# The low part of every third of the first 32 weight chunks moves from VectorE to GpSimd, in a two-layer encoder on one core

## The chip, the core and the metric
One core of a Trainium2 chip. The metric is device time in microseconds (us) of one execution; the kernel is timed in several runs and the median counts. The engines are TensorE (PE; its weight loads are PEld), VectorE (DVE), ScalarE (ACT), GpSimd (POOL) and SyncE (SP, which only issues transfers here).

## The reference
Two layers over x[256, 1024], 16 heads of 64. Both have the form x <- LayerNorm(ALPHA x + (o * silu(g)) w_out), where q, k, v and g come from one input projection.
```python
# layer 0: an indexer picks 64 keys of each query
rel   = relu(einsum('bqhd,bsd->bqhs', qi, ki) * 64 ** -0.5)
score = where(adm, einsum('bqhs,bqh->bqs', rel, wi), -inf)
_, idx = top_k(score, 64)            # softmax attention over these keys only
# layer 1: stick-breaking attention
a = where(before, exp(log_sigmoid(z) + log_stick), 0)
```
All of it is float32.

## The kernel before, in words
Every float32 operand of a large product is split in two float32r parts, a high part h (a cast) and a low part lo = src - h, and a product is three matmuls: h*h, l*h and h*l. For the weights `split` (L62) does it: ACT casts `wh` (L63), DVE subtracts `wl` (L64).

The weights come as 80 chunks of 128x1024 (512 KB) in a fixed order (`w_all`). `fetch` (L72) takes the next chunk: a DMA on SP's queue into `raw` (a pool of four, `wraw`), then the split into `wh` and `wl` (a pool of eight, `wspl`). `load_chunk` keeps `AHEAD` = 2 chunks fetched beyond the one handed out. A transfer into `raw` can start only when ACT and DVE have read the tile's earlier contents, and SP issues its transfers in order. Chunks 0 to 23 are the q, k and v projections of layer 0 (four chunks each, in the order q, k, v, k, q, v of half a matrix), 24 to 31 the gates of layer 0; then come its output projection and layer 1.

`tok_block` (L119) uses four chunks for two PSUM tiles (256 tokens by 512 columns); a chunk makes 12 matmuls of 512 columns (L107), in the order h*h, l*h, h*l, so that `wl` of a chunk is needed last. The PSUM pool `pp` has three banks. What empties them: `rope` (L191 to L198) on DVE for q and k, a copy into `vt` on ACT (L333) for v. Beside the projections run the indexer's `select` (scores `sc` on L273, from `rel` on ACT, L270; then eight rounds of MAX and MATCH_REPLACE, L279 and L280) and later the heads: `keys0` (transposes L374, then `zh` on ACT and `zl` on DVE, L229 and L230), `logits0` and so on.

The code says what is computed in which program order; a scheduler then orders the instructions of all engines by its own cost estimates. Each engine runs its instructions in that order, so an instruction that waits holds all behind it on its engine. POOL clears and casts some constants at the start (L175 to L188) and takes a power of -0.5 in each LayerNorm (L442).

Of the kernel before, what the change touches and what calls it, by code (L numbers as in the profile page):

```python
# [11 lines left out]
AF = mybir.ActivationFunctionType  # L12
# [13 lines left out]
ALPHA = (2.0 * 2) ** 0.25  # L26
# [2 lines left out]
CW = 1024  # L29
WARM = 8  # L30
AHEAD = 2
IDX_A = 5 * HD
IDX_W = IH * HD + HD + IH
NEG_ADM = -1.0e38
# [8 lines left out]
def trunk(ctx: ExitStack, tc: tile.TileContext, x_rows, x_idx, w_all, consts, lnp, out):  # L43
    nc = tc.nc
# [17 lines left out]
    def split(h, lo, src):  # L62
        nc.scalar.activation(h, src, AF.Copy)  # L63
        nc.vector.tensor_sub(lo, src, as32(h))  # L64

    # activations, feature-major: [feature in tile, tile, token], split in two float32r parts
    xTh = sb.tile([P, KT, S], F32R, name="xTh", tag="aTh")
    xTl = sb.tile([P, KT, S], F32R, name="xTl", tag="aTl")

# [3 lines left out]
    def fetch():  # L73
        c = n_chunk[0]
        if c == w_all.shape[0]:
            return
        n_chunk[0] += 1
        raw = wraw.tile([P, CW], F32, name="raw", tag="raw")
        nc.sync.dma_start(raw, w_all[c])
        wh = wspl.tile([P, CW], F32R, name="wh", tag="wh")  # L80
        wl = wspl.tile([P, CW], F32R, name="wl", tag="wl")
        split(wh, wl, raw)
        ahead.append((wh, wl))

    def load_chunk():
# [8 lines left out]
        return p.tile([P, 512], F32, name="bank", tag="bank")[:, :w]  # L94

    def load_block():
        """A quarter of [1024, 512] of a weight matrix after the other: two K tiles a chunk."""
        for _ in range(4):
            yield [w.rearrange("p (k n) -> p k n", k=2) for w in load_chunk()]

    def tok_part(outs, src, wc, c):
        """Adds a chunk's part to the token tiles in outs (tile, PSUM): the activations are stationary."""
        for xp, wp in ((0, 0), (1, 0), (0, 1)):
            for t, ps in outs:
                for k in range(2):
                    kk = 2 * c + k
                    nc.tensor.matmul(ps, src[kk][xp][:, t * P:(t + 1) * P], wc[wp][:, k, :],  # L107
                                     start=kk == 0 and xp + wp == 0, stop=kk == 7 and wp == 1)

    def tok_block(src):  # L110
        """Yields after every chunk but the last; returns the PSUM tiles."""
        ps = [bank(pp) for _ in range(NT)]
        for c, wc in enumerate(load_block()):
            if c:
                yield
            tok_part(list(enumerate(ps)), src, wc, c)
        return ps

    def mix(*gens):  # L119
        """One step of every generator in turn."""  # L120
        live = list(gens)
        while live:
            for g in list(live):
                try:
                    next(g)
                except StopIteration:
                    live.remove(g)
# [4 lines left out]
        nc.tensor.matmul(ps, sl, mh, start=False, stop=last)  # L132

    def proj_feat(ps, src, chunk):
        """[128 features, 256 tokens]: the weights are stationary."""
        w = [p.rearrange("p (k n) -> p k n", k=KT) for p in chunk]
        for wp, xp in ((0, 0), (0, 1), (1, 0)):
            for k in range(KT):
                nc.tensor.matmul(ps, w[wp][:, k, :], src[k][xp], start=k + xp + wp == 0,  # L139
                                 stop=k == 7 and wp == 1)  # L140

    # the tensor engine's clock comes up while the first loads are under way
    rest = cst.tile([P, 512], mybir.dt.bfloat16, name="rest")
    nc.vector.memset(rest, 0.0)
    idle = bank(pp)
    for _ in range(WARM):
        nc.tensor.matmul(idle, rest[:, :P], rest, start=True, stop=True)

    # ---------------------------------------------------------------- loads
    cuts = (slice(0, IDX_A), slice(IDX_A, IDX_W))  # L150
    idx_w = []
    for k in range(KT):
        raw = wraw.tile([P, CW], F32, name="raw", tag="raw")[:, :S + IDX_W]
        if k:
            nc.sync.dma_start(raw, x_idx[k])
        else:
            first = S + IDX_A
            nc.sync.dma_start(raw[:, :first], x_idx[k, :, :first])
            nc.scalar.dma_start(raw[:, first:], x_idx[k, :, first:])
        wh = wspl.tile([P, CW], F32R, name="wh", tag="wh")[:, :IDX_W]  # L160
        wl = wspl.tile([P, CW], F32R, name="wl", tag="wl")[:, :IDX_W]
# [35 lines left out]
        nc.vector.tensor_add(dst[:, :, :32], a[:, :, :32], b[:, :, 32:])  # L197
        nc.vector.tensor_add(dst[:, :, 32:], a[:, :, 32:], b[:, :, :32])  # L198

    # ---------------------------------------------------------------- layer 0: indexer  # L200
    psi = [[bank(at) for _ in range(2)] for t in range(NT)]
    for k in range(KT):
        w = idx_w[k]
# [33 lines left out]
            r = slice(i * HD, (i + 1) * HD)  # L237
            feat_split(z[0][r, i, :], z[1][r, i, :], src[r, :], scale)

    # indexer: qi of two heads stationary, ki moving, once for either head  # L240
    kz = zpad[0]
    pt = bank(at)
    for t in range(NT):
# [41 lines left out]
            negm.append(nm)  # L285


    # ---------------------------------------------------------------- layer 0: q, k
    qh = [sb.tile([P, S], F32R, name=f"qh{j}", tag=f"ah{j}") for j in range(NPAIR)]
    ql = [sb.tile([P, S], F32R, name=f"ql{j}", tag=f"al{j}") for j in range(NPAIR)]  # L290
    kr = [wk.tile([P, D], F32, name=f"kr{t}", tag="z").rearrange("p (h d) -> p h d", d=HD)
# [47 lines left out]
        yield  # L339

    def weighted_v(j, p0, p1):
        """o^T of two heads from the weights [s, (q)] of either."""
        po = bank(at)
        for i in range(2):
            hs = slice((2 * j + i) * HD, (2 * j + i + 1) * HD)
            rs = slice(i * HD, (i + 1) * HD)
            nc.tensor.matmul(po[rs, :S], vt[0][:, hs], p0(i), start=True, stop=False)  # L347
            nc.tensor.matmul(po[rs, P:S], vt[1][:, hs], p1(i), start=False, stop=True)  # L348
        if j in sg:
            gated(j, po[:, :S], sg.pop(j))  # L350
        else:
            oT[j] = keep(f"oT{j}")
            nc.scalar.activation(oT[j], po[:, :S], AF.Copy)

    def gate(j, src):
        """2 silu(g) = g (1 + tanh(g / 2)) of two heads"""
        ps = bank(pp, S)
        proj_feat(ps, src, load_chunk())
        th = wk.tile([P, S], F32, name="th", tag="og")
        nc.scalar.activation(th, ps, AF.Tanh, scale=0.5)  # L360
        if j in oT:
            nc.vector.scalar_tensor_tensor(th, th, 1.0, ps, op0=OP.add, op1=OP.mult)
            gated(j, oT.pop(j), th)
        else:
            sg[j] = keep(f"sg{j}")
            nc.vector.scalar_tensor_tensor(sg[j], th, 1.0, ps, op0=OP.add, op1=OP.mult)
# [57 lines left out]
    g_b = {}  # L424

    def out_norm(layer, x, after):
        """x[t] = LayerNorm(ALPHA x[t] + (gated o) w_out)"""
        z = [wk.tile([P, D], F32, name="z", tag="z") for _ in range(NT)]
        st = [wk.tile([P, 4, 6], F32, name="st") for _ in range(NT)]

        def residual(t, c0, ps):
            ns = slice(c0, c0 + ps.shape[1])
            nc.vector.scalar_tensor_tensor(z[t][:, ns], x[t][:, ns], ALPHA, ps, op0=OP.mult, op1=OP.add)
            for c in range(ns.start, ns.stop, 256):
                nc.vector.bn_stats(st[t][:, c // 256, :], z[t][:, c:c + 256])

        def norm(t):
            mv = wk.tile([P, 2], F32, name="mv")
            nc.vector.bn_aggr(mv, st[t].rearrange("p a b -> p (a b)"))
            rs = wk.tile([P, 1], F32, name="rs")  # L440
            nc.vector.tensor_scalar(rs, mv[:, 1:2], EPS, None, op0=OP.add)
            nc.gpsimd.tensor_tensor(rs, rs, mhalf, op=OP.pow)  # L442
            for n in range(2):
                ns = slice(n * 512, (n + 1) * 512)
                nc.vector.scalar_tensor_tensor(z[t][:, ns], z[t][:, ns], mv[:, 0:1],
                                               g_b[layer, 0][:, ns], op0=OP.subtract, op1=OP.mult)
                nc.vector.scalar_tensor_tensor(x[t][:, ns], z[t][:, ns], rs, g_b[layer, 1][:, ns],
                                               op0=OP.mult, op1=OP.add)
                after(t, n)

        tiles = [bank(pp) for _ in range(NT)]
        for c, wc in enumerate(load_block()):
            while any(k not in og for k in (2 * c, 2 * c + 1)):
                yield
            tok_part(list(enumerate(tiles)), og, wc, c)
            yield
        for t in range(NT):
            residual(t, 0, tiles[t])
        ws = list(load_block())
        for t in range(NT):  # L460
            for cols in ((0, 512),) if t == 0 else ((0, 256), (256, 512)):
                ps = bank(pp, cols[1] - cols[0])
                for c in range(4):
                    tok_part([(t, ps)], og, [w[:, :, cols[0]:cols[1]] for w in ws[c]], c)
                residual(t, 512 + cols[0], ps)
            norm(t)
        og.clear()
# [15 lines left out]
    x = [sb.tile([P, D], F32, name=f"x{t}", tag=f"x{t}") for t in range(NT)]  # L483
# [27 lines left out]
        pass  # L511
    load_gb(1)

    # ---------------------------------------------------------------- layer 1
    ys = [(yTh[:, k], yTl[:, k]) for k in range(KT)]
    wv = {}
    for t in range(NT):
# [106 lines left out]


def _rows(w):
    """[1024, n] -> [128, 8, n]: the row of a K tile in front."""
    return w.reshape(KT, P, w.shape[1]).transpose(1, 0, 2)


# [51 lines left out]
```

## Time and profile before
| | us |
|---|---|
| timed runs | 317.7, 318.9, 319.74 |
| median | 318.9 |
| span of the profiled execution (the page gives no other time of it) | 318.4 |
| PE, DVE, ACT, POOL busy in the profiled execution | 304.0, 238.5, 186.7, 7.8 |

The span is the time from the first to the last instruction of one profiled execution. Busy time of PE is modelled, so a busy PE is not PE at its peak. All times below count from the span's start. Lines are those of the kernel before; in the changed kernel lines behind the change are 2 to 6 higher (L64 is L66, L333 is L339).

### The profile page before, as it was taken

What the parts mean: (1) busy time and instruction counts of PE and PEld (TensorE: products, weight loads), DVE (VectorE), ACT (ScalarE), POOL (GpSimd) and SP (SyncE); (2) the same over time, 40 slices, a digit from 0 to 9 for tenths busy, and PEclk for the clock granted to TensorE, in tenths of its full rate; (3) what the DMA queues carried; (4) which work ended last, traced back from release to release, by engine and by line L of the source; (5) the groups of instructions that cost most, each with busy time, mean ns of one, the idle gap of its engine ahead of it and who ended that gap; (6) DMA issues with size and microseconds to landing.
All of it is one profiled execution on the core that took longest, in us unless ns stands there. A gap on an engine that the chain in (4) does not pass through costs nothing.

```text
span 318.4 us, 5179 instructions
## 1 busy us (share of the span) xinstructions
PE 304.0 (95%) x1914; PEld 264.2 (83%) x1914; DVE 238.5 (75%) x514; ACT 186.7 (59%) x365; POOL 7.8 (2%) x16
## 2 busy tenths in 40 slices
PE   8997899996999999999999999999999999999990
PEld 5985788885887899987788889999999999987790
DVE  3777999997998899897389667655677767662475
ACT  5655545664336997876306276556698888965200
POOL 3010000000000000000010100000000000000011
PEclk9999999999899999999999999999999999999997
DMA  7799744784233745665422949866543433000003
GB/s 263 249 324 307 271 141 143 236 264 153 59 95 118 258 136 153 193 203 178 134 66 80 294 134 320 282 192 165 189 148 118 110 103 118 2 1 1 2 2 130
DMA packets 14425, 50.44 MB, mean 158 GB/s; under 512 B 1600, under 2 KB 1728, under 8 KB 14400
## 3 DMA queue, kind: packets, MB, share of 16 engines
q1 hardware_dynamic: 14256, 49.97, 48.9%
q8 instruction: 15, 0.25, 0.4%
q10 hardware_dynamic: 144, 0.14, 0.1%
q14 instruction: 10, 0.08, 0.1%
HBM read 49.05 MB, written 1.05 MB: 157 GB/s over the span
## 4 chain that ended last, share of the span: by engine, by line
PE 73%; DMA 11%; DVE 10%; ACT 3%; issue 2%; DVEq 0%; SPq 0%; ACTq 0%
PE bank L139 29%; PE bank L107 28%; DMA raw<-w_all 9%; DVE wl L64 4%; PE bank L347 3%; DMA raw<-x_idx 2%; ACT wh L63 2%; PE bank L348 1%; PE bank L571 1%; PE bank L130 1%; DVE sc L280 1%; PE bank L549 1%; PE bank L548 1%; PE bank L550 1%; PE bank L132 1%
## 5 line engine op out<-in xcount | busy, mean ns | idle before, releaser
L63 ACT ACTIVATE wh<-raw 128x1024 fp32r<-128x1024 f32 (+2 forms) x89 | 90.1, 1015 | 58.9 <-DMA raw<-w_all 25.7
L64 DVE TENSOR_TENSOR wl<-raw,wh 128x1024 fp32r<-128x1024 f32 (+2 forms) x89 | 103.5, 1164 | 28.1 <-ACT wh L63 27.2
L107 PE MATMUL bank<-wh,xTh 128*128 128x512 f32 x96 | 28.6, 411 | 2.6 <-DVE rb L196 2.5
L107 PE MATMUL bank<-wh,xTl 128*128 128x512 f32 x96 | 27.9, 400 | 0.0
L107 PE MATMUL bank<-wl,xTh 128*128 128x512 f32 x96 | 27.5, 395 | 0.0
L139 PE MATMUL bank<-yTh,wh 128*128 128x256 f32 x192 | 27.4, 285 | 0.0
L139 PE MATMUL bank<-yTl,wh 128*128 128x256 f32 x192 | 26.9, 283 | 0.0
L139 PE MATMUL bank<-yTh,wl 128*128 128x256 f32 x192 | 26.9, 283 | 0.0
L139 PEld LDWEIGHTS bank<-yTh,wh 128*128 128x128 f32 x192 | 24.7, 190 | 1.2 <-DVE sl L64 0.7
L139 PEld LDWEIGHTS bank<-yTh,wl 128*128 128x128 f32 x192 | 24.8, 192 | 0.0
L139 PEld LDWEIGHTS bank<-yTl,wh 128*128 128x128 f32 x192 | 24.7, 192 | 0.0
L107 PEld LDWEIGHTS bank<-wh,xTh 128*128 128x128 f32 x96 | 17.8, 194 | 7.3 <-issue 3.6
L107 PEld LDWEIGHTS bank<-wh,xTl 128*128 128x128 f32 x96 | 18.5, 194 | 3.9
L107 PEld LDWEIGHTS bank<-wl,xTh 128*128 128x128 f32 x96 | 18.0, 188 | 3.7
L107 PE MATMUL bank<-wh,oh 128*128 128x512 f32 (+1 forms) x80 | 20.8, 355 | 0.0
L107 PE MATMUL bank<-wh,ol 128*128 128x512 f32 (+1 forms) x80 | 20.5, 352 | 0.0
L107 PE MATMUL bank<-wl,oh 128*128 128x512 f32 (+1 forms) x80 | 20.4, 350 | 0.0
L557 DVE SCALAR_TENSOR_TENSOR ab<-bank,ab 128x512 f32<-128x512 f32 (+1 forms) x16 | 8.2, 553 | 12.8 <-ACT ab L556 12.8
L107 PEld LDWEIGHTS bank<-wl,oh 128*128 128x128 f32 x80 | 14.0, 188 | 2.2
L107 PEld LDWEIGHTS bank<-wh,ol 128*128 128x128 f32 x80 | 13.9, 188 | 2.3 <-issue 0.2
L107 PEld LDWEIGHTS bank<-wh,oh 128*128 128x128 f32 x80 | 13.6, 189 | 2.2 <-issue 0.3
L398 ACT ACTIVATE p<-ml,mx 128x128 f32<-128x128 f32 (+1 forms) x32 | 14.3, 447 | 1.1 <-DVE mx L393 0.6
(148 smaller groups left out, 552.3 us busy)
## 6 DMA issues: line engine op xcount, KB each, us to landing
raw<-w_all SPq DMA_DIRECT2D x80, 512.0 KB, 4.2
raw<-x_idx SPq DMA_DIRECT2D x7, 420.0 KB, 3.9
gb<-lnp SPq DMA_DIRECT2D x4, 512.0 KB, 7.0
x<-x_rows SPq DMA_DIRECT2D x2, 512.0 KB, 6.1
y<-x SPq DMA_DIRECT2D x4, 256.0 KB, 2.1
cs<-consts SPq DMA_DIRECT2D x1, 512.0 KB, 7.0
raw<-x_idx SPq DMA_DIRECT2D x1, 288.0 KB, 3.0
raw<-x_idx ACTq DMA_DIRECT2D x1, 132.0 KB, 3.2
```

The costliest lines, as they stand in the source:

```text
L63: nc.scalar.activation(h, src, AF.Copy)
L64: nc.vector.tensor_sub(lo, src, as32(h))
L107: nc.tensor.matmul(ps, src[kk][xp][:, t * P:(t + 1) * P], wc[wp][:, k, :], start=kk == 0 and xp + wp == 0, stop=kk == 7 and wp == 1)
L130: nc.tensor.matmul(ps, sh, mh, start=first, stop=False)
L132: nc.tensor.matmul(ps, sl, mh, start=False, stop=last)
L139: nc.tensor.matmul(ps, w[wp][:, k, :], src[k][xp], start=k + xp + wp == 0, stop=k == 7 and wp == 1)
L280: nc.vector.match_replace(out=sc, in_to_replace=m8, in_values=sc, imm_value=NEG_REP)
L347: nc.tensor.matmul(po[rs, :S], vt[0][:, hs], p0(i), start=True, stop=False)
L348: nc.tensor.matmul(po[rs, P:S], vt[1][:, hs], p1(i), start=False, stop=True)
L398: nc.scalar.activation(p[:, i, :], m[:, i, :], AF.Exp, bias=mx[:, c], scale=-1.0, accum_out=sm[:, c])
L548: nc.tensor.matmul(pv, kh[:, ks], z[0][:, :, qs], start=True, stop=False)
L557: nc.vector.scalar_tensor_tensor(a, pv, 0.0, a, op0=OP.max, op1=OP.add)
```

## The change
`fetch` splits chunks 2, 5, 8, ... 29 (ten of the first 32) with the subtract on GpSimd instead of VectorE. All other chunks, and the split of activations, stay as they are.
```diff
+SHARED = 32
...
         wh = wspl.tile([P, CW], F32R, name="wh", tag="wh")
         wl = wspl.tile([P, CW], F32R, name="wl", tag="wl")
-        split(wh, wl, raw)
+        if c < SHARED and c % 3 == 2:
+            nc.scalar.activation(wh, raw, AF.Copy)
+            nc.gpsimd.tensor_sub(wl, raw, as32(wh))
+        else:
+            split(wh, wl, raw)
         ahead.append((wh, wl))
```
The scheduler lays out all engines anew. [...]
```order
L188 MEMSET zl1_178 128x512
L175 CAST cr_165<-cs_163 128x384
L442 ISA
L442 TENSOR_TENSOR rs_1918<-rs_1918,mhalf_171 128x1
L442 TENSOR_TENSOR rs_1995<-rs_1995,mhalf_171 128x1
```
Now ten subtracts stand between (chunks 2, 5, 8, 11, 14, 17 are the first six rows of L86):
```order
L194 MEMSET zl1_178 128x512
L181 CAST cr_165<-cs_163 128x384
L86 ISA
L86 TENSOR_TENSOR wl_290<-raw_287,wh_289 128x1024
L86 TENSOR_TENSOR wl_442<-raw_439,wh_441 128x1024
L86 TENSOR_TENSOR wl_552<-raw_549,wh_551 128x1024
L86 TENSOR_TENSOR wl_638<-raw_635,wh_637 128x1024
L86 TENSOR_TENSOR wl_764<-raw_761,wh_763 128x1024
L86 TENSOR_TENSOR wl_818<-raw_815,wh_817 128x1024
```
On ACT, where the first v block ends and its two PSUM banks are copied into `vt0` and `vt1`, there stood (`wh_692` is chunk 13, 763 is 14, 781 is 15, 799 is 16, 817 is 17):
```order
L63 ACTIVATE wh_692<-raw_690 128x1024
L270 ACTIVATE rel_674<-bank_670 128x512
L270 ACTIVATE rel_700<-bank_696 128x512
L63 ACTIVATE wh_763<-raw_761 128x1024
L63 ACTIVATE wh_781<-raw_779 128x1024
L333 ACTIVATE vt0_366<-bank_615 128x512
L333 ACTIVATE vt1_367<-bank_616 128x512
L270 ACTIVATE rel_722<-bank_718 128x512
```
and now stands:
```order
L65 ACTIVATE wh_692<-raw_690 128x1024
L85 ACTIVATE wh_763<-raw_761 128x1024
L276 ACTIVATE rel_648<-bank_644 128x512
L65 ACTIVATE wh_781<-raw_779 128x1024
L276 ACTIVATE rel_674<-bank_670 128x512
L276 ACTIVATE rel_700<-bank_696 128x512
L65 ACTIVATE wh_799<-raw_797 128x1024
L85 ACTIVATE wh_817<-raw_815 128x1024
L339 ACTIVATE vt0_366<-bank_615 128x512
L339 ACTIVATE vt1_367<-bank_616 128x512
L276 ACTIVATE rel_722<-bank_718 128x512
```
The casts of chunks 16 and 17 have moved ahead of the copies, and the `rel` of the second token tile's scores behind the cast of chunk 14. A little later on ACT, where the keys of the second pair of heads are split (`zh1`, first and second half), there stood (`wh_921` is chunk 20, 946 is 21, 1027 is 22, 1045 is 23):
```order
L63 ACTIVATE wh_921<-raw_919 128x1024
L229 ACTIVATE zh1_177<-bank_821 64x256
L63 ACTIVATE wh_946<-raw_944 128x1024
L229 ACTIVATE zh1_177<-bank_821 64x256
L63 ACTIVATE wh_1027<-raw_1025 128x1024
```
and now stands:
```order
L85 ACTIVATE wh_921<-raw_919 128x1024
L65 ACTIVATE wh_946<-raw_944 128x1024
L65 ACTIVATE wh_1027<-raw_1025 128x1024
L235 ACTIVATE zh1_177<-bank_821 64x256
L85 ACTIVATE wh_1045<-raw_1043 128x1024
L235 ACTIVATE zh1_177<-bank_821 64x256
```
Here too the casts of two further chunks have moved ahead of the keys' split.

## Rows read from the trace of the kernel before
**Rows 1.** The page's first part: busy us, share of the span, instructions.
```profile
PE 304.0 (95%) x1914; PEld 264.2 (83%) x1914; DVE 238.5 (75%) x514; ACT 186.7 (59%) x365; POOL 7.8 (2%) x16
```
**Rows 2.** Stretches: length, busy us of each engine, PEclk, DMA share, GB/s.
```profile
35.00:61.40 26.40, 26.40 (x123) 21.54 (x123) 26.37 (x68) 13.28 (x21) 0.00 (x0) 1.00 0.59 193
...
78.00:155.00 77.00, 76.92 (x488) 65.41 (x488) 68.09 (x198) 51.98 (x135) 0.00 (x0) 0.98 0.49 151
...
70.00:80.00 10.00, 7.52 (x33) 5.88 (x33) 8.00 (x23) 4.99 (x6) 0.00 (x0) 0.95 0.47 159
80.00:90.00 10.00, 10.00 (x42) 8.11 (x41) 9.53 (x31) 3.80 (x11) 0.00 (x0) 0.88 0.27 69
```
**Rows 3.** Waits of PE, and of DVE from 18 to 100 us: total, times, longest.
```profile
PE bank L107 <- DVE rb L196: 2.5, 1, 2.5
PE bank L130 <- issue: 1.9, 1, 1.9
...
DVE zl L230 <- ACT zh L229: 2.4, 2, 1.9
```
**Rows 4.** The chain that ended last: start, us, what.
```profile
60.72 4.55 DMA raw<-w_all
...
74.41 1.06 ACT wh L63
75.50 0.39 ACT zh L229
...
76.92 0.70 DVE rb L196
77.76 5.94 PE bank L107 x18
83.92 9.12 PE bank L107 x40
```
**Rows 5.** ACT in order of time (start, us), casts of chunk 15 and vt.
```profile
60.26 1.06 ACT L63 ACTIVATE wh<-raw 128x1024 fp32r<-128x1024 f32 x1 [0.33 <-DMA raw<-w_all]
61.23 1.09 ACT L333 ACTIVATE vt<-bank 128x512 f32<-128x512 f32 x2
```
**Rows 6.** DVE in order of time, low part of chunk 12 and the next.
```profile
57.12 1.21 DVE L64 TENSOR_TENSOR wl<-raw,wh 128x1024 fp32r<-128x1024 f32 x1
58.25 0.08 DVE L280 MATCH_VALUE_LOAD sc<-m,sc 128x8 f32 x1
```
**Rows 7.** PE in order of time, chunk 12 and the last ahead of the stop.
```profile
61.41 1.21 PE L107 MATMUL bank<-wh,xTh 128*128 128x512 f32 x4
...
74.88 0.40 PE L132 MATMUL bank<-zh,ql 128*128 128x512 f32 x1
```
**Rows 8.** POOL in order of time.
```profile
1.38 0.29 POOL L180 CAST onesr<-neg 128x128 fp32r<-128x128 f32 x1
1.61 0.53 POOL L188 MEMSET zl<- 128x512 f32 x1
...
18.59 1.47 POOL L175 CAST cr<-cs 128x384 fp32r<-128x384 f32 x1 [15.52 <-DMA cs<-consts]
...
166.36 0.92 POOL L442 TENSOR_TENSOR rs<-rs,mhalf 128x1 f32<-128x1 f32 x1 [146.30 <-DVE rs L441]
```
**Rows 9.** DVE at the times of the last two of rows 8.
```profile
18.47 1.23 DVE L64 TENSOR_TENSOR wl<-raw,wh 128x1024 fp32r<-128x1024 f32 x1 [2.11 <-ACT wh L63]
...
166.12 1.41 DVE L445 SCALAR_TENSOR_TENSOR z<-z,mv,gb 128x512 f32<-128x512 f32 x2
```
**Rows 10.** DVE groups by shape, 34 to 72 us: busy us, mean ns.
```profile
L64 DVE TENSOR_TENSOR wl<-raw,wh 128x1024 fp32r<-128x1024 f32 x15 | 18.2, 1213 | 0.0
L273 DVE SCALAR_TENSOR_TENSOR sc<-rel,wi,sc 128x256 f32<-128x256 f32 x7 | 3.3, 474 | 0.0
...
L273 DVE SCALAR_TENSOR_TENSOR sc<-rel,wi,sc 128x128 f32<-128x128 f32 x7 | 2.4, 345 | 0.0
```
**Rows 11.** Line 442 by operation, POOL's queue: times in ns, first and last start.
```profile
L442 POOLq MODIFY_POOL_CONFIG  x2: 9/9/9, 20.0 to 20.0; - x2
```

## The prediction
> **What bounds the kernel now.** I read the page first: PE is busy 95% of the span, DVE 75% [rows 1]. An average hides stages, so I went on to the stretches. From 78 to 155 us PE is busy 76.92 of 77.00 us [rows 2]: there a microsecond taken from DVE buys nothing, and every delay that PE meets earlier reaches the end whole. The waits of PE [rows 3] name what remains: 2.5 us for `rb` on DVE, and 1.9 us before L130 that "issue" hides. Then the chain [rows 4], read backwards from 77.76: PE's first matmul of the second token tile of chunk 16 needs a PSUM bank. That bank is freed by `rb`, `rb` is queued on DVE behind the second `zl`, that waits for `zh` on ACT (2.4 us in two waits, [rows 3]), and `zh` is queued behind `wh` of chunk 21, whose data lands at 74.4. That transfer could start only when DVE had read `raw` of chunk 17 (a pool of four). So up to 78 us the loop is: DVE's low part frees `raw`, the transfer lands some 4.5 us later (60.72, [rows 4]), ACT casts in its own order, and what is queued behind the cast waits. The clock is part of the price: it was granted in full until PE stood still at 75, and the slices behind show 0.95 and 0.88 [rows 2], that is 10 x 0.05 + 10 x 0.12 = 1.7 us, some of the time at the lower of the two levels.
>
> **What the change removes and adds.** Ten instructions of L64 leave DVE (chunks 2, 5, ... 29). Each occupies DVE for 1.13 us (57.12 to the next instruction at 58.25, [rows 6]). Ten subtracts of 128x1024 join POOL, which is free. What POOL takes for one no row shows. From below: 0.53 us for a MEMSET of 512 columns would be 1.06 us for 1024, without reading. From above: the CAST of 384 columns took 1.47 us, which scales to 3.92 us [rows 8]. I take the nearest row in kind, the CAST of 128 columns in 0.29 us (same types, alone): x8 = 2.34 us.
>
> **What POOL takes from DVE.** The two CASTs don't scale: 3 x 0.29 = 0.88, but 1.47 was taken, 0.6 more. The long one began at 18.59, just when DVE ran a `wl` that reads two SBUF operands from 18.47 on [rows 8, 9]. So POOL seems to be held while DVE reads two operands from SBUF. I take it that this works the other way too: a DVE instruction with two SBUF operands waits while POOL's subtract runs. Against it: `z` of L445, also with SBUF operands, kept its 0.70 us each (1.41 for two) beside a POOL instruction in flight [rows 9], though that one reads a single column. So the hold h per POOL subtract lies between 0 and 2.34 us. From 34 to 72 us `wl` and the `sc` of L273 alone, all with SBUF operands, make 18.2 + 3.3 + 2.4 = 23.9 of 38 us [rows 10]; DVE has such an instruction at its head some 63% of the time, and 0.63 x 2.34 = 1.5 us is my value. That is more than the 1.13 us saved.
>
> [...]
>
> **What the new order does.** The scheduler lays out all engines afresh, and with DVE relieved it places casts earlier. The vt copies on ACT stand behind `wh` of chunk 17 in place of chunk 15, and the second `zh` of pair 1 behind `wh` of chunk 23 in place of 21. What PE needs thus waits for data two chunks further on. The sum, step by step:
> 1. Low part of chunk 12 on DVE. Before it ends at 58.25 [rows 6]. Four instructions ahead of it are gone (chunks 2, 5, 8, 11: -4 x 1.13 = -4.5), five POOL subtracts hold DVE (2, 5, 8, 11, 14: +5 x 1.5 = +7.5): 61.25.
> 2. Only then does SP issue the transfer of chunk 16, with chunk 17 right behind it in SP's queue. It lands 4.55 us later (the one from 60.72 on, [rows 4]), two casts of 1.06 follow [rows 5], and vt stands: 61.25 + 4.55 + 2.1 = 67.9; with its own 0.55 PE goes on at 68.5. Queued behind these casts on ACT are also `rel` and `zh`, for which DVE waits in turn.
> 3. PE starts chunk 12 at 61.41 [rows 7] and has four matmuls of 0.23 us (9.12 for 40, [rows 4]) for its first token tile, for which a bank is free: at 62.3 it stands, for 68.5 - 62.3 = 6.2 us. In the trace of before the vt copies begin at 61.23 and PE doesn't wait.
> 4. PE's work from there to the second stop is as before. It was reached at 74.88 + 0.40 = 75.3 and left at 77.76. Now it is reached at 75.3 + 6.2 = 81.5. DVE gets from chunk 12 to the end of `rb` in 77.6 - 58.25 = 19.4 us in before, with the 2.4 us of waits for `zh` in it. It still has seven low parts in between (21 and 22 come, 14 and 17 go), and two holds come on top (17, 20: +3.0): 61.25 + 17.0 + 3.0 = 81.2 without, 83.6 with as many waits for data. I take the middle, 82.4. So PE goes on 82.4 - 77.76 = 4.7 us later than before.
> 5. The clock: one long stop in place of one short one, and a second short one. Between nothing and once more 1.7 us; I take 0.8.
> Sum: 4.7 + 0.8 = 5.5 us, all on PE's path. The profiled span is 318.4 us, the median of the timed runs 318.9; the page tells nothing of the profiled execution outside its span, so I add to the median: 324.4 us.
>
> At the start nothing is counted. DVE comes to `ri` 1.13 us earlier without chunk 2, and the order has spent it by moving five matmuls behind the transposes; the 1.9 us wait at L130 goes, since ACT no longer has `wh` of chunk 6 ahead of the second `qih`, but the hold by chunk 2's subtract takes about as much. After 78 us chunks 23, 26 and 29 are moved too; PE's idle there is 0.08 us, so nothing can be gained, and the cover of two chunks ahead (2 x 12 x 0.23 = 5.5 us) hides a longer subtract. If that cover fails, a hold of 1.5 us at each costs at most 4.5 us.
>
> [...]
>
> **Rivals.** *No hold, the relief counts.* POOL is only delayed itself, h = 0: chunk 12 is ready at 53.75, vt at 61.0 and PE doesn't stop at 62; `rb` of the second stop is done at 70.8 to 73.2, before PE comes at 75.3. The 2.5 us go, with them the clock's 1.7 us, and at best 1.7 of the 1.9 us at the start. Gain 2.5 + 1.7 = 4.2, at most 5.9: 314.7, down to 313.0 us. For it: L445 unslowed, and DVE busy for 26.37 of 26.40 us from 35 on [rows 2], so that relief there counts in full. Against it: the CAST. *Break-even.* Step 3 moves PE by 5h - 1.35 at the first stop and takes back 2.48 at the second, nought at h = 0.77; by step 4 (53.75 + 7h + 17.0, or 19.4 with the waits, against 77.6) nought lies at 0.64 to 0.98. If h is 0.5 to 1, which a short or shared hold would give, the time is 318.9 within 2.5 us. This h of about 0.8 is also the point from which the forecast's sign turns. *The low parts come too late on POOL,* that is, PE itself waits for `wl` of chunks 2 to 29: a subtract of 3.9 us in place of 1.13 exceeds the low part's lead of eight matmuls (1.8 us) only where the cast is not ahead, and casts run some three chunks ahead (chunk 15's at 60.26, [rows 5], PE on chunk 12 at 61.41); some 2 us more at worst, inside the forecast's range.
>
> **How the numbers follow.** The forecast (h above 1): 0.50, 324.4 us; its own range 320.5 (h near 1.1) to 329 (full hold). Break-even: 0.24, 318.9 us. Relief: 0.26, 314.7 us. One per cent, 3.2 us, is about what a measurement of this kernel can tell. Slower by more: nearly all of the first case, 0.45. Faster by more: most of the relief case and a little of the middle, 0.25. Within 1%: 0.30. The range for 8 in 10 reaches to the relief case's middle and up to near the full hold: 314 to 328.5 us.
>
> **What would show it.** Right: `wl` of L64 or `sc` of L273 longer than 1.22 and 0.47 us, or DVE idle, exactly while POOL subtracts; PE standing at about 62 us for vt with ACT on `wh` of chunk 17; a second stop near 82; clock under 1.00 behind either. Wrong: DVE's durations unchanged beside POOL, `wl` of chunk 12 before 56 us, no stop of PE at 62 and the one at 75 gone. [...]

## The result and the profile after

| | before | after |
|---|---|---|
| median of the timed runs, us | 318.3 (316.4 to 319.7) | 329.64 (328.31 to 330.51) |
| span of the profiled execution, us | 318.4 | 328.2 |
| ratio after to before | | 1.036, 95% interval 1.032 to 1.041 |

The changed kernel is 11.3 us slower; 324.4 us were forecast, with a range up to 328.5. The two profiled executions differ by 9.8 us: the one of before lies above its median (in the runs below the span is some 1.8 us shorter than the timed execution, so a span of 318.4 belongs to one of about 320.2). Ratios leave out runs that lie more than 1.5% above the fastest of the same kernel.

The page's first part, as in [rows 1]:
```profile
PE 307.6 (94%) x1914; PEld 266.2 (81%) x1914; DVE 242.0 (74%) x504; ACT 186.7 (57%) x365; POOL 32.7 (10%) x26
```
DVE has ten instructions less than before and yet is busy for 3.5 us more. Each of the ten was 1.22 us long. Something else on DVE grew, and the first question is what. (Part of the 3.5 us is only in how busy time counts: neighbours on DVE overlap by some 0.08 us, and fewer of them follow each other directly. The lengths of all instructions together grew by 0.5 us, though 12.2 us of them left.) DVE's groups by form, the low parts of before and of after (last columns: busy us, mean ns, idle before):
```profile
L64 DVE TENSOR_TENSOR wl<-raw,wh 128x1024 fp32r<-128x1024 f32 x80 | 97.3, 1217 | 27.3 <-ACT wh L63 26.6
```
```profile
L66 DVE TENSOR_TENSOR wl<-raw,wh 128x1024 fp32r<-128x1024 f32 x70 | 90.9, 1300 | 32.4 <-ACT wh L65 29.3 <-PE bank L214 2.1 <-PE bank L145 0.2
```
The same instruction became longer on average. To see which ones, POOL's subtracts in order of time (start us, us), for chunks 2, 5, 8, 11, 14, 20 and 23:
```profile
22.44 2.53 POOL L86 TENSOR_TENSOR wl<-raw,wh 128x1024 fp32r<-128x1024 f32 x1 [2.44 <-ACT wh L85]
31.48 2.40 POOL L86 TENSOR_TENSOR wl<-raw,wh 128x1024 fp32r<-128x1024 f32 x1 [6.51 <-ACT wh L85]
39.07 2.40 POOL L86 TENSOR_TENSOR wl<-raw,wh 128x1024 fp32r<-128x1024 f32 x1 [5.19 <-ACT wh L85]
48.71 3.09 POOL L86 TENSOR_TENSOR wl<-raw,wh 128x1024 fp32r<-128x1024 f32 x1 [7.24 <-ACT wh L85]
57.84 2.41 POOL L86 TENSOR_TENSOR wl<-raw,wh 128x1024 fp32r<-128x1024 f32 x1 [6.04 <-ACT wh L85]
...
74.75 2.40 POOL L86 TENSOR_TENSOR wl<-raw,wh 128x1024 fp32r<-128x1024 f32 x1 [3.14 <-ACT wh L85]
82.38 2.35 POOL L86 TENSOR_TENSOR wl<-raw,wh 128x1024 fp32r<-128x1024 f32 x1 [5.23 <-ACT wh L85]
```
and what DVE ran in the same moments, in order of time:
```profile
22.67 2.49 DVE L204 TENSOR_TENSOR ri<-ra,rb 128x160 f32<-128x160 f32 x1
...
32.42 0.69 DVE L236 TENSOR_TENSOR qil<-bank,qih 128x512 fp32r<-128x512 f32 x1 [1.23 <-ACT qih L235]
...
39.31 2.31 DVE L279 SCALAR_TENSOR_TENSOR sc<-rel,wi,sc 128x128 f32<-128x128 f32 x1
...
48.32 1.22 DVE L66 TENSOR_TENSOR wl<-raw,wh 128x1024 fp32r<-128x1024 f32 x1
...
49.66 3.22 DVE L66 TENSOR_TENSOR wl<-raw,wh 128x1024 fp32r<-128x1024 f32 x1
...
58.03 2.50 DVE L204 TENSOR_TENSOR kr<-ra,rb 128x256 f32<-128x256 f32 x1
...
75.02 3.21 DVE L66 TENSOR_TENSOR wl<-raw,wh 128x1024 fp32r<-128x1024 f32 x1
...
82.78 0.66 DVE L201 TENSOR_TENSOR ra<-bank,cs 128x512 f32<-128x512 f32 x1
```
Read the two lists side by side. The `ri` of 160 columns ends at 25.16, just behind the subtract (24.97): 2.49 us in place of 0.32. `sc` takes 2.31 us (else 0.34), `wl` 3.22 and 3.21 (else 1.21), `kr` 2.50 (else 0.41). In each case DVE's instruction has two SBUF operands, begins after POOL's and ends about its own length behind it (0.13 to 0.19 us less). At 48.71 it is the other way round: `wl` had begun at 48.32, and POOL's subtract takes 3.09 us, 0.69 more than its 2.40. Beside chunk 5 and chunk 23 DVE ran `qil` and `ra`, which read one operand from PSUM, and these kept 0.69 and 0.66 us. So the hold is real, in both directions, and it lasts until the other instruction ends. The excess, subtract by subtract from chunk 2 to 29: 2.17, 0, 1.97, 2.01, 2.09, 0.79, 2.00, 0, 1.64 and 0, together 12.7 us, against 10 x 1.13 = 11.3 us that left.

On balance DVE thus lost little more than a microsecond. That PE lost ten follows from where the holds lie. The waits of PE, as in [rows 3]:
```profile
PE bank L113 <- DVE rb L202: 6.1, 3, 3.2
PE bank L250 <- DVE ri L224: 3.4, 1, 3.4
PE bank L113 <- ACT vt L339: 1.2, 1, 1.2
...
PE bank L311 <- DVE rq L204: 1.2, 1, 1.2
```
In before there were a wait of 2.5 us for `rb`, the 1.9 us of "issue" and 1.0 us for `ri`. Now there are six stops, 11.9 us in all. The chain that ended last, as in [rows 4], passes through the long instructions one after the other:
```profile
22.75 2.40 DVE ri L204
...
26.58 0.48 PE bank L250
...
39.31 2.31 DVE sc L279
...
49.74 3.14 DVE wl L66
...
58.11 2.42 DVE kr L204
...
62.04 1.14 DVE wl L66
63.24 0.33 SPq L81
63.67 4.39 DMA raw<-w_all
...
69.04 1.06 ACT vt L339 x2
...
84.78 0.70 DVE rb L202
85.62 1.91 PE bank L113 x6
...
96.61 2.85 DVE wl L66
...
100.93 1.40 PE bank L113 x5
```
Here stand the stations that the forecast named: the low part of chunk 12 on DVE (62.04), the transfer that it lets go (63.67), vt (69.04), `rb` (84.78) and PE behind it (85.62; 77.76 in before). The last part of the accounting is the clock, in the stretches as in [rows 2] (length, busy PE, PEld, DVE, ACT, POOL, then PEclk):
```profile
20.00:30.00 10.00, 6.61 (x25) 4.99 (x24) 9.29 (x22) 4.38 (x5) 2.53 (x1) 0.77 0.85 281
30.00:40.00 10.00, 10.00 (x47) 8.29 (x46) 7.08 (x11) 7.01 (x12) 3.33 (x2) 0.89 0.66 214
...
80.00:90.00 10.00, 6.78 (x25) 5.16 (x25) 9.84 (x28) 2.50 (x3) 2.35 (x1) 0.84 0.62 224
90.00:100.00 10.00, 9.54 (x43) 7.54 (x41) 8.52 (x23) 5.70 (x13) 2.49 (x1) 0.99 0.23 63
...
78.00:155.00 77.00, 72.39 (x457) 61.72 (x456) 65.16 (x190) 49.21 (x122) 7.23 (x3) 0.98 0.45 139
```
The first two of these stretches in before were:
```profile
20.00:30.00 10.00, 8.97 (x45) 7.11 (x44) 8.91 (x24) 5.93 (x7) 0.06 (x1) 1.00 0.85 268
30.00:40.00 10.00, 8.08 (x42) 6.33 (x41) 8.56 (x18) 5.79 (x11) 0.00 (x0) 1.00 0.83 290
```
PE stood for 3.4 us up to 26.6 and for 3.2 us up to 85.6, and around each the granted clock is below full: 10 x (0.23 + 0.11) = 3.4 us at the start, where before had none, and 10 x (0.16 + 0.01) = 1.7 us around 85, as much as before had around 78. From 78 to 155 us PE is busy for 72.39 of 77 us, where before had 76.92: that stretch is no longer full.

### The profile page after: what moved, and what is told of

Read it like the earlier page. It is cut to its first block, busy times and chain, and to the rows that moved or that the text cites. A ratio compares the mean times of both kernels' runs of the same rounds, so it can differ in the third digit from the quotient of the medians.

```text
span 328.2 us, 5218 instructions
## 1 busy us (share of the span) xinstructions
PE 307.6 (94%) x1914; PEld 266.2 (81%) x1914; DVE 242.0 (74%) x504; ACT 186.7 (57%) x365; POOL 32.7 (10%) x26
## 3 DMA queue, kind: packets, MB, share of 16 engines
HBM read 49.05 MB, written 1.05 MB: 153 GB/s over the span
## 4 chain that ended last, share of the span: by engine, by line
PE 72%; DVE 15%; DMA 6%; issue 3%; ACT 2%; SPq 0%; DVEq 0%; ACTq 0%
PE bank L145 28%; PE bank L113 28%; DVE wl L66 5%; DMA raw<-w_all 3%; PE bank L353 3%; DMA raw<-x_idx 2%; DVE sc L279 2%; PE bank L136 1%; PE bank L354 1%; PE bank L577 1%; DVE sc L286 1%; DVE ra L201 1%; DVE m L285 1%; PE bank L138 1%; DVE rb L202 1%
## 5 line engine op out<-in xcount | busy, mean ns | idle before, releaser
L66 DVE TENSOR_TENSOR wl<-raw,wh 128x1024 fp32r<-128x1024 f32 (+2 forms) x79 | 97.1, 1232 | 33.2 <-ACT wh L65 30.0
L65 ACT ACTIVATE wh<-raw 128x1024 fp32r<-128x1024 f32 (+2 forms) x79 | 79.5, 1009 | 58.1 <-PE bank L113 26.6
L113 PE MATMUL bank<-wh,xTh 128*128 128x512 f32 x96 | 30.4, 424 | 7.4 <-DVE rb L202 6.1
L86 POOL TENSOR_TENSOR wl<-raw,wh 128x1024 fp32r<-128x1024 f32 x10 | 24.9, 2485 | 67.1 <-ACT wh L85 58.1
L113 PEld LDWEIGHTS bank<-wh,xTh 128*128 128x128 f32 x96 | 18.1, 200 | 12.7 <-issue 7.7
L113 PE MATMUL bank<-wl,xTh 128*128 128x512 f32 x96 | 28.2, 405 | 0.0
L448 POOL TENSOR_TENSOR rs<-rs,mhalf 128x1 f32<-128x1 f32 x4 | 3.8, 957 | 207.7 <-DVE rs L447 207.7
```

The lines of the kernel that those rows point to most:

```text
L86: nc.gpsimd.tensor_sub(wl, raw, as32(wh))
```

## The experiments

The theory: while POOL reads SBUF, an instruction of DVE with two SBUF operands waits for the whole length of POOL's, and what falls on DVE's way to `ri`, `rq`, `vt` and `rb` stops PE. The rivals: the new order (casts of two further chunks ahead of vt and zh) costs the time; POOL's writing costs it; the start alone costs it, or the late chunks; or `raw`, which comes free only when POOL too has read it, lets the transfers start late. Ratios are to the kernel before in the same comparison, with 95% intervals.

**Without the subtract.** `e1_none` uses the high part in place of the low one in the ten chunks, so the low part is left out; `e2_memset` lets POOL write as long as it subtracted, without reading.
```diff
-            nc.gpsimd.tensor_sub(wl, raw, as32(wh))
+            wl = wh
```
```diff
-            nc.gpsimd.tensor_sub(wl, raw, as32(wh))
+            for _ in range(3):
+                nc.gpsimd.memset(as32(wl), 0.0)
```
Expected of e1_none: 

> For the ten chunks nobody forms a low part: the high part stands in for it, so that the DVE relief of the change stays and POOL does nothing (the output's precision suffers). Hold theory (POOL's subtract and a DVE instruction with two SBUF operands shut each other out, and this is what costs): 311 to 317 us, DVE's sc of L279 all under 0.5 us, no stop of PE over 2 us between 20 and 100 us. Order theory (the new order, with casts two chunks further ahead of vt and zh, is what costs): still 322 us or more, with PE standing near 60 and 75 to 85 us.

Expected of e2_memset: 

> As the changed kernel, but POOL fills the low part of the ten chunks with zeros by three MEMSETs (about 2.9 us together), so it writes as long as the subtract took and reads nothing. If the hold comes from POOL's reading: DVE's two-operand instructions keep their lengths (sc 0.34, wl 1.21 us) and the time is within 1.5 us of e1_none. If any use of SBUF by POOL holds DVE: DVE instructions of 2 us and more beside the MEMSETs and 325 us or more.

Measured: e1_none 316.66 us, ratio 0.993 [0.990, 0.996]; e2_memset 316.51 us, 0.995 [0.992, 0.998]. With the low parts simply gone from DVE the kernel is 0.7% faster, and with MEMSETs in their place 0.5%: more the relief is not worth here. And POOL busy for as long as in after takes none of it back. DVE's groups of e2_memset, 20 to 120 us:
```profile
L66 DVE TENSOR_TENSOR wl<-raw,wh 128x1024 fp32r<-128x1024 f32 x24 | 29.1, 1218 | 1.8 <-ACT wh L65 1.7
L280 DVE SCALAR_TENSOR_TENSOR sc<-rel,wi,sc 128x256 f32<-128x256 f32 x7 | 3.3, 476 | 0.9 <-ACT rel L277 0.9
...
L225 DVE COPY ri<-ri 128x64 f32<-128x64 f32 x2 | 0.9, 468 | 0.0
```
`wl` and `sc` have their usual 1218 and 476 ns beside 28.9 us of MEMSETs, so POOL's writing doesn't hold them. The copy of `ri` within SBUF is another matter: 468 ns on average where it takes 186 in before (one of the two took 0.75 us, the other began between two MEMSETs). So a copy, with a single operand, is held by a mere write, and so is a pair of multiplications of `p` by one number a row (1.39 us at 95.43, where it takes 0.60 at 109.02 in after).

**POOL reads one operand.** `e5_copy` copies `raw` to `wl`; the subtraction of the high part is left out.
```diff
-            nc.gpsimd.tensor_sub(wl, raw, as32(wh))
+            nc.gpsimd.tensor_copy(wl, raw)
```
Expected: 

> GpSimd copies raw to wl in place of subtracting (one SBUF operand is read; the high part is not subtracted, so the product leaves that out). Theory 'a GpSimd instruction that reads SBUF holds VectorE's two-operand instructions for its whole length': wl, ri, sc, kr beside a copy are longer by what is left of the copy, as beside a subtract; with a copy of 2.3 us the time is as after's, 327 to 331 us, and in proportion less where the copy is shorter (a copy of 1.2 us: 319 to 324). Rival 'only a GpSimd instruction that itself reads two SBUF operands holds VectorE': lengths as in the kernel before (wl 1.22, sc 0.34 and 0.47 us), time as with the three MEMSETs, 315 to 318 us.

Measured: 317.12 us, 0.997 [0.994, 1.000]. The time alone would speak for the rival; the lines don't. POOL's first copy and three instructions of DVE in order of time:
```profile
21.57 1.92 POOL L86 CAST wl<-raw 128x1024 fp32r<-128x1024 f32 x1 [1.17 <-DMA raw<-w_all]
```
```profile
22.50 1.16 DVE L203 TENSOR_TENSOR ri<-ra,rb 128x160 f32<-128x160 f32 x1
...
39.95 1.02 DVE L279 SCALAR_TENSOR_TENSOR sc<-rel,wi,sc 128x128 f32<-128x128 f32 x1
...
84.50 1.05 DVE L409 TENSOR_SCALAR p<-p,rc 128x256 f32<-128x256 f32 x2
```
`ri` and `sc` are held, by what is left of a copy, and so is the pair of `p`, a multiplication by one number a row (0.60 us for such a pair at 109.02 in after, with POOL idle up to 109.55, 1.05 here). A copy that isn't held itself takes 1.04 to 1.06 us, so the holds are short: some 4 us in all against 11.3 us saved. A POOL instruction that reads one SBUF operand holds too, `ri` by 0.84 and `sc` by 0.68 us; the rival's first half falls. But the 319 to 324 us expected for so short a copy were too high: with DVE relieved by some 7 us in sum, the time lies between that of e1_none and that of before.

**The hold alone, in the old order.** `e7_both` leaves all low parts on DVE, and POOL does the ten subtracts once more into a tile that nobody reads. The order of DVE and PE is that of before.
```diff
+        split(wh, wl, raw)
         if c < SHARED and c % 3 == 2:
-            nc.scalar.activation(wh, raw, AF.Copy)
-            nc.gpsimd.tensor_sub(wl, raw, as32(wh))
-        else:
-            split(wh, wl, raw)
+            junk = cst.tile([P, 512], mybir.dt.bfloat16, ...)
+            for n in range(2):
+                ns = slice(n * 512, (n + 1) * 512)
+                nc.gpsimd.tensor_sub(junk, raw[:, ns], as32(wh)[:, ns])
```
Expected: 

> VectorE keeps all its low parts; GpSimd does the subtract of the ten chunks once more, as two halves of 512 columns into a tile that nobody reads. VectorE and TensorE have the order of the kernel before. Theory 'the hold is the cost': ten holds of 1.0 to 2.4 us join and nothing is saved, so VectorE has 10 to 20 us more; TensorE stops at 10 to 45 us more than in after by up to 11 us: 326 to 336 us. Rival 'the new order (casts of two further chunks ahead of vt and zh) is the cost': the order is the old one, so 317 to 320 us.

Measured: 326.04 us, 1.024 [1.020, 1.028]. DVE and PE run in the old order, nothing waits for POOL's result (only `raw` and `wh` come free when POOL too has read them, as in after), and 2.4% are lost. PE's waits, and DVE's low parts:
```profile
PE bank L114 <- DVE rb L203: 4.3, 1, 4.3
PE bank L251 <- DVE ri L225: 3.0, 2, 2.4
PE bank L312 <- DVE rq L205: 1.3, 1, 1.3
```
```profile
L66 DVE TENSOR_TENSOR wl<-raw,wh 128x1024 fp32r<-128x1024 f32 x80 | 101.5, 1270 | 26.6 <-ACT wh L65 25.9
```
The stops for `ri`, `rq` and `rb` are there as in after, and `rb` of the second stop costs 4.3 in place of 2.5 us. So the new order isn't needed for the loss. Nor does it harm by itself, as far as the runs reach: in e1_none and e2_memset vt stands behind the cast of chunk 19 and in e5_copy behind that of 18 (15 in before, 17 in after), the second `zh` of pair 1 behind that of chunk 23, as in after, and none of the three is slower than before. After's order to the letter without any hold was not tried. Nor can the times of e7_both and after be set against each other for the order's share: e7_both has halves, and keeps all low parts on DVE.

The late release of `raw` was not tested by itself. In after SP's queue waits for L86 eight times, 21.9 us in all, but the chain that ended last has no piece of POOL there, in e7_both or in e8_halves. In e11_midsix (below) it has one: POOL's subtract at 72.83 (2.42 us), then a transfer, a cast and `zl` ahead of `rb`. So in that kernel this path was the last to release `rb`, and what share it has in the loss is not shown.

**Shorter holds.** `e8_halves` cuts each subtract in two of 512 columns; the other engines keep after's order. The question is whether DVE gets in between the halves.
```diff
-            nc.gpsimd.tensor_sub(wl, raw, as32(wh))
+            for n in range(2):
+                ns = slice(n * 512, (n + 1) * 512)
+                nc.gpsimd.tensor_sub(wl[:, ns], raw[:, ns], as32(wh)[:, ns])
```
Expected: 

> As after, but each subtract on GpSimd is two instructions of 512 columns; the orders of the four other engines are those of after. [...] Rival 'what counts is the sum of GpSimd's reading time, however it is cut': two holds of 1.2 us for one of 2.4, 328 to 331 us, as after.

Measured: ratio 1.017 [1.010, 1.023]; the runs behind it took 322.57, 325.19 and 326.71 us. A fourth took 327.72 and is not in the ratio; the median of all four is 325.95, 1.026 of that of before, below the 328 to 331 us of the rival. All four lie below the four of after (328.31 to 330.51), with the same work on the same engines, so halves lose less, but how much less is not sharp. DVE beside chunk 14, which is to be compared with the `kr` of 2.50 us in after:
```profile
55.83 1.47 DVE L206 TENSOR_TENSOR kr<-ra,rb 128x256 f32<-128x256 f32 x1
...
57.48 1.25 DVE L281 SCALAR_TENSOR_TENSOR sc<-rel,wi,cs 128x256 f32<-128x256 f32 x1
```
`kr` is held by 1.06 us, then comes a short stretch of MATCH instructions, then `sc` is held by 0.8. DVE gets in between the halves, and no instruction is held by more than 1.1 us. Twelve instructions of DVE were held, 10.4 us in all against 12.7 in after.

**Which subtracts cost.** Five kernels differ in source only in which chunks go to POOL (the scheduler orders each anew, so a step from one to the next holds that too):
```diff
-        if c < SHARED and c % 3 == 2:
+        if c == 2:                            # e4_only_first
+        if 20 < c < SHARED and c % 3 == 2:    # e6_late
+        if c in (8, 11, 14, 17):              # e9_middle
+        if 2 < c < 23 and c % 3 == 2:         # e11_midsix
+        if 2 < c < SHARED and c % 3 == 2:     # e3_not_first
```
Expected of e4_only_first: 

> POOL forms the low part of chunk 2 only. If the start is what was missed: 321 to 325 us, PE standing about 3.4 us for ri near 26 us with the clock down behind it. If it is swallowed later: 317.5 to 320 us.

Expected of e6_late: 

> Only chunks 23, 26 and 29 are subtracted on GpSimd, the orders of TensorE and SyncE are those of the kernel before. Theory 'a hold costs only where VectorE is the bound or near it, and behind 78 us TensorE is': each of the three holds some 2 us of VectorE, TensorE's waits grow by less than 1 us, 317 to 320 us. Rival 'the third stop of after (1.39 us at 100.9) and the low clock behind it come from the late subtracts themselves': TensorE stands some 1.4 us at 95 to 102 us here too, with the clock behind it 320 to 323 us.

Expected of e9_middle: 

> Only chunks 8, 11, 14 and 17 are subtracted on GpSimd; the start and all behind 72 us are left to VectorE. Theory 'the holds between 35 and 72 us are what TensorE pays for, each about 2 us against 1.13 us saved': four holds of 0.8 to 2.1 us, 6.5 to 8 us, against 4.5 us saved, so TensorE leaves its second stop 2 to 4 us later than in the kernel before: 320 to 323 us. Rival 'the loss needs the late start too, without it these holds are slack': 317 to 319 us. Rival 'it is these four alone': 326 us or more.

Expected of e11_midsix: 

> Chunks 5, 8, 11, 14, 17 and 20 are subtracted on GpSimd; against e3_not_first the chunks 23, 26 and 29 go back to VectorE. Theory 'the last three cost only where VectorE is already late, because the third stop and the clock behind it come from them': the stop near 99 us goes, 324 to 326 us against 328.0 of e3_not_first. Rival 'the last three cost nothing here either, as in e6_late; the third stop is what the second one left behind': 327 to 329 us with the stop still there.

Expected of e3_not_first: 

> POOL forms the low part of chunks 5, 8, ... 29 only; chunk 2 stays on DVE. If the start is what the forecast missed (PE stood 3.4 us for ri at 26.6, and 3.4 us of clock went between 20 and 40 us): 321 to 325 us, clock 1.00 from 20 to 40 us. If the loss at the start is swallowed by the later stops, which come from DVE alone: 327 us or more.

| chunks on POOL | us | ratio to before | 95% interval |
|---|---|---|---|
| 2 (e4_only_first) | 317.39 | 0.999 | 0.995 to 1.002 |
| 23, 26, 29 (e6_late) | 318.06 | 1.001 | 0.998 to 1.004 |
| 8, 11, 14, 17 (e9_middle) | 322.42 | 1.012 | 1.005 to 1.018 |
| 5, 8, 11, 14, 17, 20 (e11_midsix) | 326.42 | 1.024 | 1.018 to 1.029 |
| 5 to 29 (e3_not_first) | 327.98 | 1.030 | 1.022 to 1.039 |
| all ten (after) | 329.64 | 1.036 | 1.032 to 1.041 |

The first subtract alone and the last three alone cost nothing that can be measured, the six of the middle cost 2.4%. The steps from e11_midsix to e3_not_first and on to after are 0.6% each, about 2 us; as intervals they overlap, so each is likely rather than shown, but the step over both, 1.024 to 1.036, lies outside. So what was expected of e3_not_first and e4_only_first if the start were the whole of what was missed, 321 to 325 us, did not come in either: most of the loss at the start is swallowed by later stops. What remains of it shows in the trace of e3_not_first, where the low part of chunk 12 ends at 61.17 in place of 63.09 and PE leaves the second stop at 83.65 in place of 85.62. Two lines tell why the same subtract costs nothing alone. PE's instructions in e4_only_first, each with what it waited for:
```profile
25.86 0.33 PE L250 MATMUL bank<-cs,ri 128*128 128x128 f32 x1 [3.06 <-DVE ri L224]
...
77.28 0.70 PE L113 MATMUL bank<-wh,xTh 128*128 128x512 f32 x2 [0.56 <-DVE rb L202]
```
Here too PE stands for 3.06 us at the start, but arrives later at the second stop and waits there for 0.56 us in place of 2.48: the same stretch is waited for once. In after DVE is late at the second stop as well, so PE pays at both. As for the last three, here is the third stop in e3_not_first:
```profile
98.74 0.70 PE L113 MATMUL bank<-wh,xTh 128*128 128x512 f32 x2 [1.36 <-DVE rb L202]
```
In e11_midsix, with the same stop of 3.23 us at 83.7, PE doesn't stand again before 110 us; in e6_late, with the three late subtracts, it doesn't either. The third stop needs both, a DVE that is already late and another hold. (In e11_midsix, with the same second stop, PE leaves it some 6 us later than in before: that much is the middle's.) The time of e11_midsix, 326.42, came out a little above the 324 to 326 that I had expected. In e9_middle the time is as expected, though not by the way: in the profiled execution, the fastest of its runs, PE stands for vt for 1.91 us at 65.3 and then no more for `rb`.

**The other way round: POOL casts.** A copy on POOL that isn't held takes only 1.05 us, so I let POOL make the high part and left every subtract on DVE, for the ten chunks (`e10_cast`) and for chunks 14, 17, 20 and 23 (`e12_midcast`).
```diff
-            nc.scalar.activation(wh, raw, AF.Copy)
-            nc.gpsimd.tensor_sub(wl, raw, as32(wh))
+            nc.gpsimd.tensor_copy(wh, raw)
+            nc.vector.tensor_sub(wl, raw, as32(wh))
```
Expected of e10_cast: 

> GpSimd makes the high part of the ten chunks (a cast, one SBUF operand, 1.05 us in e5_copy) in place of ScalarE, and VectorE keeps every low part. Theory 'what a GpSimd instruction costs is its length times the share of the time in which VectorE has an instruction from SBUF at its head': ten holds of 0.3 to 0.9 us, 3 to 7 us, nothing saved on VectorE, but ScalarE has ten casts of 1.06 us less ahead of zh and rel, so the waits for zh (2.4 us) go in part: 317 to 321 us. Rival 'ScalarE's casts ahead of zh set the stops': 314 to 316.5 us, a version that beats both. Rival 'the low part waits for a slower cast': over 322 us.

Expected of e12_midcast: 

> GpSimd makes the high part of chunks 14, 17, 20 and 23 alone (a cast of 1.05 us in place of ScalarE's 1.06), so that e10_cast's loss at the start (2.06 us for ri, 1.1 and 0.6 for rq) cannot come. Theory 'GpSimd's casts relieve ScalarE ahead of zh, and four short holds cost VectorE under 2.5 us in all': the stop for rb near 78 us falls from 2.48 to 1.1 us or less, as in e10_cast, 315.5 to 317.5 us, a little faster than the kernel before. Rival 'what is won at zh is lost in holds, as in e10_cast': 317.5 to 319.5 us, no difference.

Measured: e10_cast 319.63 us, 1.003 [1.000, 1.007]; e12_midcast 318.76 us, 1.004 [1.001, 1.007]. Neither beats the kernel before, and the 315.5 to 317.5 us expected of e12_midcast did not come. PE's stop for `rb` near 78 us did become shorter, in e12_midcast:
```profile
76.95 0.70 PE L113 MATMUL bank<-wh,xTh 128*128 128x512 f32 x2 [1.21 <-DVE rb L202]
90.06 0.70 PE L113 MATMUL bank<-wh,xTh 128*128 128x512 f32 x2 [0.54 <-DVE rb L202]
```
1.21 in place of 2.48 us, as hoped, but half a microsecond comes back at 90, and DVE beside the casts is held again (`sc` 0.99 in place of 0.47, `kr` 1.27 in place of 0.41). No version found here is faster than before while it does all the work, and even with ten low parts gone e1_none gained only 0.7%.

## Why the prediction was right and wrong

In short: the hold was forecast rightly, but what it costs was counted at the middle alone. What failed is "At the start nothing is counted" and the cover of chunks 23, 26 and 29 behind 78 us: these two cost some 2 us each. The middle was sized too low as well: its six subtracts cost 7.5 us in e11_midsix, where the whole sum was 5.5.

*Right: the hold and its size.* The forecast took 1.5 us per subtract, as 63% of 2.34 us. Measured from chunk 2 to 14 it was 8.24 us for five (7.5 forecast), over all ten 1.27 us each. It isn't a smooth share, though: but for one of 0.79 us a subtract costs DVE some 2 us or nothing, as a two-operand instruction comes up early or not at all. The length, 2.40 us where POOL isn't held itself, came out as forecast (2.34), but by luck: the row was scaled from a CAST of 128 columns in 0.29 us, and a CAST of 1024 takes not 2.34 but 1.04 us (e5_copy). The two-operand subtract happens to be that much longer. The first of the ten, chunk 2's, took 2.53 us, 0.13 more. Ahead of it POOL's queue ran the MODIFY_POOL_CONFIG of [rows 11] (at 19.9 and 20.0 in after, 8 ns each), and the 2.44 us for which POOL then stood idle ended with ACT's cast; what else might lie in them doesn't show. That the CAST of 384 columns had been held was read rightly: in e8_halves, where DVE ran only instructions with a PSUM operand beside it, it took 0.50 in place of 1.47 us.

By the kind of POOL's instruction: beside MEMSETs, which only write, `wl` kept 1218 ns (e2_memset), beside subtracts it took 3.2 us (after), and beside a copy, which reads one operand, `ri` took 1.16 in place of 0.32 us (e5_copy). The copy of `ri` took 468 in place of 186 ns on average beside MEMSETs, and the pair of `p`, 0.60 us alone, took 1.05 beside a copy and 1.39 beside MEMSETs. Why MEMSETs hold these two and not `wl`, no trace shows.

*Step 1, chunk 12 at 61.25.* Measured 61.96 + 1.13 = 63.09, that is 1.84 later. 0.74 of it are holds. The other 1.1 us is DVE idle: from 20 to 40 us it was idle for 0.71 + 2.92 = 3.6 us, against 1.09 + 1.44 = 2.5 us in before, and it waits there for `qih` and `zh` of ACT, which had itself waited 4.75 us for PE's transposes: PE, standing and at the lower clock, handed over the indexer's results late. In e3_not_first, without chunk 2 on POOL, DVE is idle for 0.8 us in these stretches, the clock is at 1.00 and chunk 12 ends at 61.17. This is the first failed step: **"At the start nothing is counted."** The forecast set the earlier `ri` against the hold of chunk 2 and let both end there. But PE stood for 3.39 us at L250 (1.03 in before), the clock took 3.4 us more, and the lateness came back to DVE. It reached PE's second stop as some 2.0 us (85.62 against 83.65 in e3_not_first).

*Steps 2 and 3, vt and the stop at 62.* The chain runs as described (wl, transfer of 4.39 us, two casts, vt), and vt starts at 69.04 (67.9 forecast), PE goes on at 69.68 (68.5). The stop itself is 1.22 us, not 6.2: PE came late already, from the stops at 26.6, 42.6 and 54.7 and the low clock behind the first, which the forecast didn't have. The lateness was right, its division into stops wrong. And the new order has a smaller part in it than the text gave it: e7_both loses 2.4% in the old one, and e1_none, with vt two casts further back still, loses nothing.

*Step 4, `rb` and PE at 82.4.* Measured: `rb` ends at 85.39, PE goes on at 85.62, 7.9 us later than in before; 4.7 were forecast. 1.84 of the difference come from step 1; 1.15 from DVE's way from chunk 12 to `rb`, 22.3 us, for which the text gave 20.0 to 22.4 and took the middle (in e3_not_first it is 22.2 too, so this term was too small whatever the start did); the last 0.2 lie between `rb` and PE.

*Step 5, the clock, and all behind 78 us.* Around the second stop the clock takes 1.7 us, as in before, so the 0.8 forecast there did not come; the 3.4 us at the start, which did, are inside the lateness of step 1. The second failed step is **"After 78 us ... nothing can be gained"** with its cover of 5.5 us against a longer subtract. The subtract's own length is covered indeed, PE never waits for a `wl` of POOL. But the hold fell on DVE's other work: `wl` beside chunk 26 took 2.85 us, and PE stood for 1.39 us for `rb` at 100.9. From the second stop's 7.9 and the third's 1.4 us, 9.3 of the 9.8 us between the spans are found. Against the forecast's 5.5 that is 3.2 us more at the second stop, 1.4 at the third and 0.5 that are not found, less the 0.8 of the clock.

So sign and mechanism of the likeliest case held, and the price was too low in three terms. By the ratios the six subtracts of the middle cost 7.5 us (1.024), chunks 23 to 29 some 2.0 (1.024 to 1.030) and chunk 2 some 1.9 (1.030 to 1.036), where the forecast had 5.5 in all, with some 0.4 for chunk 2 in it and nothing for the late ones. The rest of the difference in the medians comes from the executions: the waits were read from one of about 320.2 us, low clock around 78 us included, and the sum was added to a median of 318.9. The upper end of the range stopped short: it reached near a full hold in the middle (324.4 + 5 x (2.34 - 1.5) = 328.6 us), and the 4.5 us named for a failed cover behind 78 us were not in it. No run shows a full hold by each of the five: in after they held DVE for 8.24 us, 1.65 each, and the longest for 2.17.

*The rivals.* No hold: the relief itself exists, but at 0.7% (e1_none) it is worth half of the 4.2 us that the text gave it. Break-even at a hold of 0.8: e5_copy, whose ten copies held for some 0.4 us each, comes out at 0.997, on the side of the relief. Low parts too late on POOL: not seen, no wait of PE for `wl` of L86.

## What to carry to other kernels

Before moving work from DVE to POOL, list what DVE will run beside it: in these runs only instructions with two SBUF operands (`wl` 3.2 us in place of 1.21), copies within SBUF (`ri` 0.75 in place of 0.19) and multiplications within SBUF by one number a row (a pair of `p` 1.05 and 1.39 in place of 0.60) were held, the two-operand ones beside a subtract until it ended (`ri` to 25.16, the subtract to 24.97). A move that took 1.13 us off DVE and held it for about 2 us lost where PE waited for DVE behind the holds (1.024 in e11_midsix; 1.001 in e6_late, where it did not), and shorter POOL instructions lost less than long ones (1.017 in e8_halves, 1.026 with its fourth run, against 1.036 in after). And a stop of PE that a later slack swallows today (3.06 us in e4_only_first, at 0.999) is not free once that slack is gone: count the holds at the start and at the end together with those in the middle.

## What the runs showed of the hardware that was not expected

- The hold is nearly all or nothing: of the ten subtracts of after, about 2.40 us each, three held DVE for nothing, one for 0.79 us, six for 1.64 to 2.17 us.
- A one-operand fp32 copy within SBUF (186 ns) was held by POOL's MEMSET, which reads nothing (0.75 us in e2_memset; the other of the two copies began between two MEMSETs and kept 0.18), while two-operand subtracts beside the same MEMSETs kept 1218 ns.
- On POOL a cast of 1024 columns took 1.04 us (e5_copy, and e12_midcast at 77.01), one of 384 took 0.50 (e8_halves) and one of 128 took 0.29 [rows 8]: by an estimate from these three about 0.18 us and 0.84 ns a column. A subtract of 1024 columns with two operands took 2.40 us (after).
- Leaving out ten DVE instructions of 1.13 us each, some of them from a stretch in which DVE is busy for 26.37 of 26.40 us [rows 2], made the kernel only 2.2 us faster: in e1_none, at a clock of 1.00 from 20 to 120 us, PE still stood 2.4 us for `rb`, 1.2 for `ri` and 0.8 for `wh`.
